# Two FFN projections of a hybrid decoder step as seven half-depth block products (Strassen's scheme)

## The chip, the cores and the metric

The kernel runs on one core of a Trainium2 chip. A core has a matrix engine (TensorE, in the profile PE, with its weight loads as PEld), a vector engine (DVE), an activation engine (ACT), a general engine (POOL), and a queue engine (SP) that issues nearly all transfers here. Each engine takes its instructions in the order in which the program emits them. The metric is the device time of one execution in microseconds, the median of several runs.

## The reference, cut to what matters

The step takes 2048 prompt tokens and 32 sample tokens through one layer: a mixer (an S5 scan and gated linear attention), then a gated FFN with a short causal convolution. The change touches the FFN alone (x has 1024 columns, D_FF is 2816, all float32):

```python
    x = x + jnp.concatenate([y5, o], axis=-1) @ w_o

    h2 = rms_norm(x, ffn_norm)
    a, b = jnp.split(h2 @ w_up, 2, axis=-1)
    ext = jnp.concatenate([conv0.astype(a.dtype), a], axis=1)
    a_conv = conv_b
    for w in range(CONV_W):
        a_conv = a_conv + conv_w[w] * ext[:, w:w + T]
    x = x + (jax.nn.silu(a_conv) * b) @ w_down
    ...
    y_prompt = rms_norm(xp, final_norm)
```

## The kernel before

Every float32 operand of a matmul is held as the sum of a high and a low part on a shorter grid, and every product is three matmuls: high by high, high by low, low by high (`Acc.mm3`). The splitting is vector work: ACT or POOL copies the high part, DVE or POOL subtracts it for the low part.

The program emits a main stream of matmul blocks and, between them, steps of generators that stand in the background (`Background.tick`, `drain`). A coarse clock of the program's own decides only where a step is put; what is emitted is a fixed order for each engine. SBUF is shared out as 43 large slots and 6 small ones (`Slots`); a background generator starts only when enough slots are open.

Four windows of 512 tokens go through the mixer (PSUM banks `mm`, background banks `bg`). The S5 mixer works by halves of 1024 tokens and four groups of channels. When the FFN begins, the S5 of the second half is still to be done: four scans (`gen_s5`), then a gate for pairs of chunks (`gen_glu`, data through the DRAM arrays `ydT` and `gdT`), then the output projection in two halves of columns (`gen_wo`, from `x1d` to `x2d`, eight tiles and a sample tile each). These run in the background of the FFN's first half; all FFN sums and these use the banks `all`.

The FFN of before runs by halves of the tokens. `x2_slots` takes 16 slots (when 17 are open) for the normalized, transposed and split activations `X2H`, `X2L`, which `gen_build` makes tile by tile while the first FFN blocks already run. `FORDER` then goes over the 22 column blocks of D_FF: `ffn_up` makes a and b for a block (8 contraction tiles by 3 matmuls each, windows of 512 tokens in the first half, 352 in the second), convolves and gates; after every second block `ffn_down` adds that pair's share of the down projection to the residual `x2`, which stays in SBUF:

```python
            a = Acc(pa[:, :n], 3 * KD)
            for k in range(KD):
                a.mm3(wv(ab[0], 0, k), wv(ab[0], 1, k), X2H[k][:, s:e], X2L[k][:, s:e])
```

The work of the second half's S5 must be over before the last two blocks of the first half (`bg.drain(*s5[1], *stages[1])`), and `gen_finish` norms and stores the tiles at the end.

Of the kernel before, what the change touches and what calls it, by code (L numbers as in the profile page):

```python
# [124 lines left out]
class Share:  # L125
    """slots that a generator has set aside, so that it can run to its end"""
# [19 lines left out]
def _names(x):  # L146
    """the parts of a tile that x touches"""
# [14 lines left out]
class Free:  # L162
    """a wait for the last use of a tile, not for its data"""
# [5 lines left out]
class Banks:  # L169
    """a wait for the next n background banks"""  # L170
# [5 lines left out]
class Clock:  # L176
    """A coarse estimate of when each engine is free and each tile is written; it only orders the
    instruction streams."""
# [14 lines left out]
    def span(x):  # L193
        """is x in DRAM, its tensor, its first and its last element"""
# [3 lines left out]
    def split_tile(self, t, period, edges):  # L198
        """track parts of the columns of a tile"""
# [5 lines left out]
    def reuse(self, key, t):  # L205
        """a new tile in the place of an old one"""
# [73 lines left out]
class Engine:  # L280
    """nc.<engine> with every call noted in the clock"""
# [56 lines left out]
class Background:  # L338
    """Generators whose steps are set between the blocks of the main matmul stream. A step yields
    what its successor waits for: tiles that TensorE reads, an engine whose backlog counts, or  # L340
    "idle" for something that another part of the program has yet to emit."""
# [14 lines left out]
    def when(self, e):  # L356
        """the time at which the step of e may start"""
# [18 lines left out]
    def relieve(self):  # L376
        """a step that may free memory for the main stream"""
# [6 lines left out]
    def start(self, g, n):  # L384
        """the first n steps of a generator"""
# [4 lines left out]
    def need(self, slots, n):  # L390
        """run steps until n slots are free that nobody has set aside"""
# [3 lines left out]
    def tick(self, most=None):  # L395
        """steps that are ready, for at most so much of TensorE's time"""
# [14 lines left out]
    def drain(self, *gs):  # L411
        """run the generators to their end, others in their waits"""
        while any(e[3] is g for e in self.gens for g in gs):
            if self.tick(1.0):
                continue
            for e in sorted(self.gens, key=lambda e: (self.when(e), e[0], e[1])):
                if self.run(e):
                    break
            else:
                raise RuntimeError("stuck")  # L420
# [3 lines left out]
def kernel(ctx: ExitStack, tc: tile.TileContext, ins, outs):  # L424
# [32 lines left out]
    gdT = drp.tile([2, 4, P, 8, NCH], F32, tag="gdT", name="gdT")  # L457
    x1d = drp.tile([TP + NSMP, D], F32, tag="x1d", name="x1d")
    x2d = drp.tile([TP + NSMP, D], F32, tag="x2d", name="x2d")

# [5 lines left out]
    kept = set()         # banks of sums that the background must go round  # L466
# [7 lines left out]
    clock.next_banks = next_banks  # L474

# [1807 lines left out]
```

## Time and profile before

| | |
|---|---|
| median of 3 runs | 2483.21 us (2483.13 to 2484.64) |
| span of the profiled execution | 2482.2 us |
| PE busy | 2380.4 us, 96% |
| PE weight loads busy | 2032.0 us, 82% |
| DVE busy | 1392.0 us, 56% |
| ACT busy | 678.7 us, 27% |
| POOL busy | 667.5 us, 27% |
| chain that ended last | PE 74%, DVE 7%, POOL 5%, ACT 3% |

The profiled execution is within 1 us of the median. All calls of an engine go through one helper, so every instruction stands under line 290; groups are told apart by the names of tiles (`t_L` a large slot, `t_H` a small one, `pair_L` half of a large one, `all`, `mm` and `bg` PSUM banks) and by shapes. The mean duration of a matmul holds its way through the pipeline; what a matmul of a long row costs is its group's busy time divided by its count.

### The profile page before, as it was taken

The page shows a single profiled execution, that of the slowest core. Times are in us where ns is not written, and L with a number is a line of the kernel's source. Part 1 is how long each engine was busy: PE and PEld are TensorE (multiplying, and loading weights), DVE is VectorE, ACT ScalarE, POOL GpSimd, SP SyncE. Part 2 cuts the span into 40 slices and gives each one's busy share as a digit, 9 for nine tenths or more (in the row PEclk, how much of TensorE's full clock was granted, in tenths as well). Part 3 has the DMA queues.
Part 4 walks back from the last instruction along what each step waited for, and adds up shares of the span by engine and source line. Part 5 has one row for each costly group of instructions (what it writes and reads, how often), then busy time and mean ns, then how long its engine had stood idle before and what let it go on. Part 6 is the DMA issues. An engine that isn't in the chain of part 4 may idle for free.

```text
span 2482.2 us, 32287 instructions
## 1 busy us (share of the span) xinstructions
PE 2380.4 (96%) x12363; PEld 2032.0 (82%) x12363; DVE 1392.0 (56%) x2652; ACT 678.7 (27%) x1401; POOL 667.5 (27%) x761
## 2 busy tenths in 40 slices
PE   7898999899999998999999999999999999999998
PEld 5677777677877877788888888878999999999997
DVE  7677457765633555554445444457555555555555
ACT  3242244444422622223421111154111111111113
POOL 5255325545402344541111001113111011111112
PEclk9889999989999999999999999999999999999999
DMA  6135455427454522233233311136111111111111
GB/s 166 60 96 139 134 152 166 124 86 222 134 178 126 206 77 55 65 94 103 76 113 125 109 51 51 43 101 209 43 43 52 49 37 51 45 41 51 44 34 74
DMA packets 272793, 237.35 MB, mean 96 GB/s; under 512 B 46242, under 2 KB 219482, under 8 KB 272640
## 3 DMA queue, kind: packets, MB, share of 16 engines
q1 hardware_dynamic: 272288, 235.15, 31.5%
q8 instruction: 97, 1.59, 0.3%
q14 instruction: 56, 0.46, 0.1%
q10 hardware_dynamic: 352, 0.15, 0.0%
HBM read 189.16 MB, written 46.09 MB: 95 GB/s over the span
## 4 chain that ended last, share of the span: by engine, by line
PE 74%; DVE 7%; POOL 5%; ACT 3%; issue 1%; DMA 1%; SPq 0%; POOLq 0%; DVEq 0%; ACTq 0%
PE all L290 56%; PE mm L290 11%; PE bg L290 8%; DVE t_L L290 3%; DVE t_H L290 3%; POOL t_H L290 2%; ACT t_L L290 2%; DVE pair_L L290 2%; POOL t_L L290 1%; ACT t_H L290 1%; POOL pair_L L290 1%; POOL rr L290 0%; ACT L290 0%; SPq L290 0%; DMA pair_L<-in_x_prompt_dram 0%
## 5 line engine op out<-in xcount | busy, mean ns | idle before, releaser
L290 PE MATMUL all<-t_L,t_L 128*128 128x512 f32 (+3 forms) x7936 | 1571.2, 360 | 11.2 <-DVE t_L L290 7.5
L290 PEld LDWEIGHTS all<-t_L,t_L 128*128 128x128 f32 x7936 | 1376.3, 187 | 195.2 <-DVE t_L L290 10.2
L290 POOL TENSOR_SCALAR t_L<-t_L 128x1024 fp32r<-128x1024 f32 (+1 forms) x179 | 233.4, 1309 | 1077.8 <-PE all L290 638.1
L290 PE MATMUL mm<-t_L,t_L 128*128 128x512 f32 (+2 forms) x2160 | 494.8, 386 | 18.2 <-DVE t_L L290 14.9
L290 PEld LDWEIGHTS mm<-t_L,t_L 128*128 128x128 f32 (+1 forms) x2160 | 385.2, 192 | 104.4 <-issue 19.5
L290 DVE TENSOR_TENSOR t_L<-t_L,all 128x512 f32<-128x512 f32 (+1 forms) x374 | 249.5, 683 | 168.9 <-PE all L290 158.3
L290 DVE TENSOR_TENSOR t_L<-t_L,t_L 128x1024 fp32r<-128x1024 f32 (+1 forms) x192 | 249.9, 1320 | 48.1 <-POOL t_L L290 24.6
L290 DVE SCALAR_TENSOR_TENSOR t_H<-all,cw,t_H 128x351 f32<-128x351 f32 (+4 forms) x222 | 140.7, 634 | 137.0 <-ACT t_H L290 136.2
L290 ACT ACTIVATE t_H<-all,cw 128x352 f32<-128x352 f32 (+3 forms) x111 | 77.1, 695 | 370.0 <-PE all L290 369.8
L290 DVE TENSOR_TENSOR t_H<-t_H,all 128x352 f32<-128x352 f32 (+3 forms) x112 | 65.5, 585 | 178.2 <-PE all L290 150.9
L290 DVE TENSOR_TENSOR t_L<-t_H,t_L 128x512 fp32r<-128x512 f32 (+5 forms) x171 | 96.3, 579 | 108.4 <-ACT t_L L290 73.3
L290 ACT ACTIVATE t_L<-t_H 128x512 fp32r<-128x512 f32 (+3 forms) x155 | 80.8, 531 | 223.8 <-DVE t_H L290 181.7
L290 ACT ACTIVATE t_H<-t_H 128x352 f32<-128x352 f32 (+4 forms) x113 | 62.1, 550 | 272.2 <-DVE t_H L290 215.3
L290 POOL TENSOR_TENSOR t_L<-t_L,t_L 128x1024 fp32r<-128x1024 f32 x44 | 118.3, 2691 | 44.4 <-ACT t_L L290 32.5
L290 ACT ACTIVATE t_L<-t_L 128x1024 fp32r<-128x1024 f32 (+5 forms) x104 | 95.4, 932 | 62.4 <-DVE t_L L290 30.5
L290 PE MATMUL bg<-t_L,t_L 128*128 128x512 f32 (+6 forms) x604 | 103.9, 339 | 2.3 <-DVE t_H L290 2.3
L290 PEld LDWEIGHTS bg<-t_L,t_L 128*128 128x128 f32 (+3 forms) x604 | 81.3, 184 | 22.0 <-issue 8.4
L290 ACT ACTIVATE t_H<-all 32x512 f32<-32x512 f32 (+1 forms) x26 | 14.9, 575 | 239.1 <-PE all L290 239.1
L290 ACT ACTIVATE t_L<-bg 128x512 fp32r<-128x512 f32 (+6 forms) x118 | 52.6, 466 | 90.1 <-PE bg L290 87.5
L290 ACT ACT_TABLE_LOAD x43 | 55.2, 1283 | 50.4 <-DVE aprev L290 31.5
L290 ACT ACTIVATE t_H<-t_L 128x1024 bf16<-128x1024 f32 (+2 forms) x59 | 57.2, 974 | 34.9 <-DVE t_L L290 23.8
L290 POOL TENSOR_SCALAR rr<-ss 128x1 f32<-128x1 f32 (+1 forms) x51 | 25.0, 490 | 143.0 <-ACT t_H L290 137.8
(173 smaller groups left out, 1646.4 us busy)
## 6 DMA issues: line engine op xcount, KB each, us to landing
t_L<-in_w_up_dram SPq DMA_DIRECT2D x88, 512.0 KB, 4.2
t_L<-in_w_in_dram SPq DMA_DIRECT2D x64, 512.0 KB, 4.9
t_L<-in_w_down_dram SPq DMA_DIRECT2D x44, 512.0 KB, 3.3
t_L<-in_w_o_dram SPq DMA_DIRECT2D x24, 512.0 KB, 5.0
t_L<-x2d SPq DMA_DIRECT2D x24, 512.0 KB, 4.5
out_dram<-t_L SPq DMA_DIRECT2D x17, 512.0 KB, 2.7
t_L<-in_x_prompt_dram SPq DMA_DIRECT2D x16, 512.0 KB, 6.5
t_H<-gdT SPq DMA_DIRECT2D x24, 256.0 KB, 4.1
```

The costliest lines, as they stand in the source:

```text
L290: r = fn(*args, **kw)
```

## The change

The FFN is rewritten. The prompt and sample tokens are cut into three chunks of 704, 704 and 672 columns (`CH`), each chunk into two halves of tokens and the model width into two halves; the weight block of a and b is the other two-by-two matrix. Seven products of half depth (4 contraction tiles, 12 matmuls of 352 or 336 columns) take the place of eight, in the order `PO`; two accumulate on banks of earlier ones. The up projection runs over all 22 blocks of each chunk first; gated rows are stored to the DRAM array `gT`. Then the down projection runs in four parts of the contraction (4, 6, 6, 6 blocks of D_FF) over eight pairs of token tiles, with the residual read from and written to `x2d` in each part.

The last fence of the diff's hooks (`p == 5`) is that of the down projection, where `G` is POOL. Operands are sums and differences of blocks. Those of the activations (up) and of w_down (down) are 21 held slots (`R`), made once for a chunk or part; those of the other side are made for each block (`Item.step`).

```diff
-        hi, lo = ([S.get("L", F32R) for _ in range(KD)] for _ in range(2))
-        for i in half_tiles(0):
-            build[i] = bg.add(3, gen_build(i))
+            bg.need(S, 29)
+        if R or S.open() < 29:
+            return
+        for p in PO:
+            R[p] = [S.get("L", F32R) for _ in range(3)]
+        bg.start(bg.add(3, gen_raw(0)), 1)
+        for i in chunk_tiles(0):
+            build[0, i] = bg.add(3, gen_build(0, i))
+        build["first"] = bg.add(3, gen_first_chunk())
...
+    W.share.end()
+    FW = Share(S, 12.0)
+    FS = Share(S, 4.0)
+    KH = (2, 3, 3, 3)
+    K0 = (0, 4, 10, 16)
+    items = [("up", c, fb) for c in range(3) for fb in range(NF)]
+    items += [("down", q, j) for q in range(4) for j in range(8)]
...
+            if at == 0:
+                self.pair(ra, 1, 2)
+            elif at == 1:
+                ew(self.s[:, h : 2 * h], rb[:, :h], rb[:, h : 2 * h], ALU.add)
+                ew(self.s[:, :h], self.s[:, h : 2 * h], ra[:, :h], ALU.subtract)
+            elif at == 2:
+                self.pair(self.s, 6, 5)
+            elif at == 3:
+                ew(self.s[:, :h], ra[:, h : 2 * h], self.s[:, :h], ALU.subtract)
+                ew(self.s[:, h : 2 * h], ra[:, :h], rb[:, :h], ALU.subtract)
+            elif at == 4:
+                self.pair(self.s, 3, 7)
...
+    def products(it, hook, part, n, kh, out, tail=None):
+        for p in PO:
+            wh, wl, _ = it.take(p)
+            if p in (1, 6, 5, 7, 3):
+                B[p] = bank("up", True)
+            b = B[{2: 1, 4: 7}.get(p, p)]
+            for k in range(kh):
+                for w_, x_ in ((wh, xh), (wh, xl), (wl, xh)):
+                    lh, rh = (w_[:, c], x_) if out == "w" else (w_[:, c], x_)
+                    PE.matmul(b[:, :n], lh, rh, start=i == 0 and p not in (2, 4), stop=i == n_ - 1, skip_group_check=p in (2, 4))
+            if tail:
+                tail(p)
+            after(lambda p=p: hook(p, B))
+            prepare()
+            bg.tick()
...
+            elif p == 5:
+                add(Vv, U, B[5])
+                add(r2[:, hi], r2[:, hi], Vv, G)
+                add(r1[:, hi], r1[:, hi], Vv, G)
+                add(r2[:, lo], r2[:, lo], U, G)
...
+    bg.drain(*(build.pop(k) for k in list(build)))
+    for n, (kind, c, j) in enumerate(items):
+            if j == NF - 1:
+                bg.drain(*(s5[1] + stages[1] if c == 0 else []), *nxt)
+                last = next_window(c + 1) if c < 2 else next_operands(0)
+            up(it, last)
```

`ew` puts an elementwise operation on DVE or POOL by the program's clock, `split2` makes the high part on ACT and the low part with `ew`, `tail` makes the next chunk's or part's operand of a product when the last block has used the old one.

The change also sets another order at the places below. The first is PE at the FFN's start. Before: `mm` is the mixer's last sum, rows with `ident` are transposes that build activations, `all_7016` is the first FFN product.

```order
L290 MATMUL mm_6923<-t_L_6817,t_L_6657 128x512
L290 MATMUL bg_6939<-ident,t_L_6806 128x128 x4
...
L290 MATMUL bg_6979<-ident,t_L_6811 128x128 x4
L290 MATMUL all_7016<-t_L_6666,t_L_6823 128x384
...
L290 MATMUL all_7016<-t_L_6669,t_L_6824 128x384
L290 MATMUL all_7030<-ident,t_L_6869 128x128 x4
L290 MATMUL all_7043<-ident,t_L_6869 128x128 x4
L290 MATMUL all_7016<-t_L_6670,t_L_6823 128x384
```

PE at the same place in the changed kernel, where the first product is `all_7114`:

```order
L290 MATMUL mm_6826<-t_L_6742,t_L_6656 128x512
L290 MATMUL all_6900<-ident,t_L_6824 128x128 x4
L290 MATMUL all_6909<-ident,t_L_6824 128x128 x4
...
L290 MATMUL all_6998<-ident,t_L_6980 128x128 x4
L290 MATMUL all_7016<-ident,t_L_7007 128x128 x4
L290 MATMUL all_7025<-ident,t_L_7007 128x128 x4
L290 MATMUL all_7114<-t_L_6780,t_L_6861 128x352
L290 MATMUL all_7114<-t_L_6781,t_L_6861 128x352
```

Before, the transposes of later tiles stood between the matmuls of the first product; now those of all six tiles of the first chunk stand ahead of it.

The second place is SP's queue at the gate of the second half's S5 (`ydT` is read, `gdT` written). Before:

```order
L290 DMA t_L_9328<-ydT 128x4x256
L290 DMA gdT<-t_L_9328 128x4x256
L290 DMA t_L_9497<-ydT 128x4x256
L290 DMA t_L_9525<-in_w_up_dram 128x8x128
L290 DMA t_L_9531<-in_w_down_dram 128x1024
L290 DMA gdT<-t_L_9497 128x4x256
L290 DMA t_L_9659<-ydT 128x4x256
L290 DMA t_L_9789<-in_w_down_dram 128x1024
L290 DMA t_L_9795<-in_w_up_dram 128x8x128
L290 DMA gdT<-t_L_9659 128x4x256
```

SP at the same place in the changed kernel:

```order
L290 DMA t_L_10608<-ydT 128x4x256
L290 DMA gdT<-t_L_10608 128x4x256
L290 DMA t_L_10681<-ydT 128x4x256
L290 DMA gdT<-t_L_10681 128x4x256
L290 DMA t_L_10754<-ydT 128x4x256
L290 DMA gdT<-t_L_10754 128x4x256
L290 DMA t_L_10827<-ydT 128x4x256
L290 DMA gdT<-t_L_10827 128x4x256
L290 DMA t_H_10900<-ysd 32x512
```

The FFN's weight loads that stood between the gate's transfers are gone from there; each load of `ydT` still stands behind the store of the block ahead.

The third place is PE at that gate. Before: `all_9376` and `all_9429` are gate sums, the rows of 512 columns are FFN products.

```order
L290 MATMUL all_9368<-t_L_9255,t_L_9129 128x512
L290 MATMUL all_9376<-t_L_9354,t_L_9294 128x256
...
L290 MATMUL all_9376<-t_L_9354,t_L_9301 128x256
L290 MATMUL all_9404<-t_L_9122,t_L_8947 128x512
...
L290 MATMUL all_9420<-t_L_9255,t_L_9129 128x512
L290 MATMUL all_9429<-t_L_9354,t_L_9294 128x256
```

PE in the changed kernel, from the end of block 20 of the first chunk (`all_10353`) to block 21 (`all_11547`); `all_10446` belongs to the last S5 group, `all_10616` and `all_10689` to the gate, `all_11350` to the last output projection, rows with `ident` to the second chunk's activations:

```order
L290 MATMUL all_10353<-t_L_6799,t_L_10289 128x352
L290 MATMUL all_10446<-t_L_10378,t_H_10380 128x128 x4
...
L290 MATMUL all_10616<-t_L_10610,t_L_10598 128x256
...
L290 MATMUL all_10677<-ones,t_H_10614 128x1 x2
L290 MATMUL all_10689<-t_L_10683,t_L_10598 128x256
...
L290 MATMUL all_11350<-t_L_11158,t_L_11346 64x512
L290 MATMUL all_11379<-ident,t_L_11370 128x128 x4
...
L290 MATMUL all_11531<-ident,t_L_11513 128x128 x4
L290 MATMUL all_11547<-t_L_6780,t_L_10338 128x352
```

Before, FFN products stood between the sums of the gate and of the output projection; now none stands between the two blocks, and the last S5 group, the whole gate, the whole output projection and six tiles of building do.

## Rows read from the trace of the kernel before

**Rows 1.** Busy time by windows: length, PE, PEld, DVE, ACT, POOL, PEclk, DMA, GB/s

```profile
835.00:2472.00 1637.00, 1611.43 (x8283) 1420.58 (x8283) 874.61 (x1680) 372.38 (x742) 311.22 (x406) 0.99 0.23 71
...
1700.00:2400.00 700.00, 700.00 (x3937) 652.83 (x3936) 376.30 (x786) 117.02 (x246) 88.83 (x72) 1.00 0.18 55
```

**Rows 2.** Groups by shape, PE: count, busy us, mean ns, idle before

```profile
L290 PE MATMUL all<-t_L,t_L 128*128 128x512 f32 x4320 | 993.7, 390 | 6.8 <-DVE t_L L290 6.8
L290 PE MATMUL all<-t_L,t_L 128*128 128x352 f32 x3168 | 508.1, 322 | 0.0
...
L290 PE MATMUL all<-t_L,t_L 128*128 128x256 f32 x240 | 32.0, 292 | 3.5 <-DVE aprev L290 3.3
```

**Rows 3.** DMA issues: count, KB each, median us to landing

```profile
t_L<-in_w_o_dram SPq DMA_DIRECT2D x24, 512.0 KB, 5.0
t_L<-x2d SPq DMA_DIRECT2D x24, 512.0 KB, 4.5
...
t_H<-gdT SPq DMA_DIRECT2D x24, 256.0 KB, 4.1
...
t_L<-ydT SPq DMA_DIRECT2D x8, 512.0 KB, 5.8
```

**Rows 4.** Timeline of SP, 1150 to 1235 us: start, duration, instruction

```profile
1154.24 0.37 SPq L290 DMA_DIRECT2D gdT<-t_L  x1
...
1174.15 0.37 SPq L290 DMA_DIRECT2D gdT<-t_L  x1
...
1229.03 0.36 SPq L290 DMA_DIRECT2D gdT<-t_L  x1
```

**Rows 5.** Groups by shape, DVE, ACT and POOL

```profile
L290 DVE TENSOR_TENSOR t_L<-t_L,t_L 128x1024 fp32r<-128x1024 f32 x180 | 236.0, 1330 | 43.7 <-POOL t_L L290 24.6 <-ACT t_L L290 19.1
...
L290 POOL TENSOR_TENSOR t_L<-t_L,t_L 128x1024 fp32r<-128x1024 f32 x44 | 118.3, 2691 | 44.4 <-ACT t_L L290 32.5 <-PE bg L290 9.6
...
L290 ACT ACTIVATE t_L<-t_L 128x1024 fp32r<-128x1024 f32 x49 | 59.2, 1222 | 26.4 <-DMA t_L<-in_w_in_dram 16.0 <-DVE t_L L290 5.4 <-DMA t_L<-ydT 3.9
...
L290 DVE TENSOR_TENSOR t_L<-t_H,t_L 128x512 fp32r<-128x512 f32 x66 | 47.5, 733 | 33.9 <-ACT t_L L290 33.8
...
L290 ACT ACTIVATE t_L<-t_H 128x512 fp32r<-128x512 f32 x66 | 40.3, 629 | 119.1 <-DVE t_H L290 77.3 <-DMA t_H<-gdT 35.0 <-PE all L290 5.9
...
L290 DVE TENSOR_TENSOR t_H<-t_H,all 128x352 f32<-128x352 f32 x66 | 34.4, 522 | 91.8 <-PE all L290 90.5 <-ACT t_H L290 1.3
...
L290 DVE SCALAR_TENSOR_TENSOR t_H<-all,cw,t_H 128x351 f32<-128x351 f32 x44 | 25.5, 579 | 64.5 <-ACT t_H L290 64.5
...
L290 DVE SCALAR_TENSOR_TENSOR t_H<-all,rrn,t_H 128x512 f32<-128x512 f32 x16 | 12.0, 751 | 48.0 <-PE all L290 48.0
```

**Rows 6.** Timeline of all engines, 812 to 850 us

```profile
835.09 0.44 PE L290 MATMUL all<-t_L,t_L 128*128 128x384 f32 x1 [0.20 <-ACT t_L L290]
...
838.62 1.22 ACT L290 ACTIVATE t_H<-t_L 128x1024 bf16<-128x1024 f32 x1
...
842.97 1.04 ACT L290 ACTIVATE t_H<-t_L 128x1024 bf16<-128x1024 f32 x1
```

**Rows 7.** Timeline of POOL, 850 to 930 us

```profile
860.01 0.89 POOL L290 TENSOR_TENSOR t_H<-t_L,t_L 128x128 f32<-128x128 f32 x2 [10.88 <-ACT t_L L290]
...
868.05 2.09 POOL L290 TENSOR_SCALAR t_L<-t_L 128x1024 fp32r<-128x1024 f32 x2
...
900.47 0.52 POOL L290 TENSOR_TENSOR t_L<-t_L,t_H 128x128 f32<-128x128 f32 x1
```

**Rows 8.** Busy time by windows near the start, columns as in rows 1

```profile
60.00:70.00 10.00, 0.22 (x1) 0.00 (x0) 7.61 (x23) 6.33 (x9) 1.45 (x1) 0.74 0.46 157
70.00:80.00 10.00, 9.06 (x31) 7.30 (x32) 9.93 (x9) 1.89 (x2) 9.85 (x5) 0.75 0.05 6
```

**Rows 9.** Timeline of DVE, 855 to 912 us

```profile
864.51 0.67 DVE L290 TENSOR_TENSOR t_H<-t_L,t_L 128x128 f32<-128x128 f32 x2
...
868.12 2.19 DVE L290 TENSOR_TENSOR t_H<-t_L,t_L 128x128 f32<-128x128 f32 x2 [2.19 <-POOL t_L L290]
```

More of the change, by code (lines that the diff above doesn't have):

```diff
@@ L1174, in gen_s5 @@
             yield "idle"
-        while live[0] >= s5_width[0] or S.open() < 6.5 or (hf and not X2L):
+        while live[0] >= s5_width[0] or S.open() < 6.5 or (hf and not R):
             yield "idle"
@@ L1645, in rows_of, with spans, ew, split2 @@
         return (TP, NSMP) if i == 16 else (i * P, P)
-    def h2_transpose(t, rows, col):
+    def spans(c, i):
+        r0, r = rows_of(i)
+        c0, n = CH[c][0], width(c)
+        out = []
+        for j in range(2):
+            lo, hi = max(r0, c0 + j * n), min(r0 + r, c0 + j * n + n)
+            if lo < hi:
+                out.append((lo - r0, hi - lo, j, lo - c0 - j * n))
+        return out
+    def ew(out, a, b, op):
+        n = 1
+        for d in out.shape[1:]:
+            n *= d
+        e = V if max(clock.eng["V"], clock.eng["PE"]) + 0.07 + 1.04e-3 * n <= max(clock.eng["G"], clock.eng["PE"]) + 0.12 + 2.15e-3 * n else G
+        tt(out, a, b, op, e)
+    def split2(hi, lo, src):
+        act(hi, src, AF.Copy)
+        ew(lo, src, f(hi), ALU.subtract)
+    def gen_raw(c):
+        while (c == 1 and not all(("p3", h, 1, j) in flags for h in (1, 2) for j in [16] + list(range(8)))) or raw or S.open() < 7.0:
+            yield "idle"
+        raw.extend(S.get("L") for _ in range(6))
+        for t in raw:
+            clock.split_tile(t, SL, (0, XN, 2 * XN, 3 * XN, SL))
+    def gen_build(c, i):
+        r0, r = rows_of(i)
+        while not raw or ("split", c - 1) not in flags or not all(("p3", h, int(i > 7), j) in flags for h in (1, 2) for j in ([16] if i == 16 else range(8))) or S.open() < 2.0:
+            yield "idle"
+        S_ = Share(S, 1.5)
+        t = S_.get("M")
+        SP.dma_start(t[:r, :D], x2d[r0 : r0 + r])
+        yield t
+        yield from norm_tile(t[:r, :D], t[:r, :D], r, None, S_)
+        yield t, Banks()
         for q in range(2):
@@ L1685, with gen_operands, gen_first_chunk @@
+    def gen_operands(c):
+        for p in PO:
+            operand(p, width(c), 4, xpc, rawx)
+            yield "V"
+        S.put(*raw)
+        raw.clear()
+        flags.add(("split", c))
+    def gen_first_chunk():
+        yield from gen_diff(0)
+        yield from gen_operands(0)
     p3 = [0]
@@ L2065 @@
     bg.most = MOST[4]
[L2066 to L2082 removed]
+    bg.drain(conv)
@@ new lines, with load_item, prepare @@
+    live_items, loaded = [], [0]
+    def load_item():
+        if loaded[0] < len(items) and len(live_items) < 3 and FW.left >= 2.0 and S.whole() >= 2:
+            it = Item(loaded[0])
+            it.load()
+            live_items.append(it)
+            loaded[0] += 1
+    def prepare():
+        for it in live_items[:2]:
+            if it.at < 6:
+                if FW.left >= it.need() and S.whole() >= it.need():
+                    it.step()
+                break
+        load_item()
@@ new lines, in up, with yp_, gen_raw_down @@
+        products(it, hook, xpc, n, 4, "w", last)
+    def yp_(p, k, r, n):
+        return R[p][k][:, 512 * r : 512 * r + 512]
+    def gen_raw_down(q):
+        while raw or S.open() < 7.0:
+            yield "idle"
+        kh = KH[q]
+        raw.extend(S.get("L") for _ in range(2 * kh))
+        for k, t in enumerate(raw):
+            clock.split_tile(t, SL, (0, 512, SL))
+            SP.dma_start(t[:, :D], w_down[(K0[q] + k) * P : (K0[q] + k + 1) * P, :])
+        for k in range(kh):
+            yield raw[k], raw[kh + k]
+            b12, b22 = (raw[i * kh + k][:, 512:1024] for i in range(2))
+            ew(b12, b22, b12, ALU.subtract)
@@ L2222, in conv_states @@
         S.put(*co)
[L2224 to L2249 removed]
+    for _ in range(2):
+        load_item()
@@ L2250 @@
+    after()
     bg.drain(*ends)
```

515 lines of the change are left out of this document (322 added, 193 removed).

## The prediction

> **What bounds the kernel now.** I read the busy time by windows first. From the first FFN product at 835 us [rows 6] to the last at 2472 us PE is busy 1611 of 1637 us, and from 1700 to 2400 us all of the time, with DVE at 54%, ACT at 17% and POOL at 13% [rows 1]. So the FFN is bound by PE's work; the other engines have room, and the 26 us in which PE was idle there lie where the second half's S5 still runs beside the FFN. Then I read the groups by shape for what a matmul costs: 993.7 / 4320 = 0.230 us for 512 columns, 508.1 / 3168 = 0.160 for 352, 32.0 / 240 = 0.133 for 256 [rows 2]. Last, since the change takes away the cover of what ran in the background, I read the timelines of that work.
>
> The sum is made against the span, 2482 us; the median of the runs is 1 us longer.
>
> **PE's work: -180 us.** Before, the FFN's products are 2016 (up) and 2112 (down) matmuls of 512 columns, 3168 of 352, 96 of 384 (0.175 each, an estimate by columns between the 352 and 512 rows) and 48 of 256: 949 + 508 + 17 + 6 = 1481 us. After, each of 66 up blocks has 7 x 12 = 84 matmuls: 3696 of 352 and 1848 of 336 (0.153, by columns from the 352 row), and the down projection has 8 x 7 x 3 x (2 + 3 + 3 + 3) = 1848 of 512: 593 + 283 + 425 = 1301 us. The sample's 112 small matmuls become 110. This is 12% of the products, and no waiting can make it larger.
>
> **The start of the FFN: +35 us.** The held slots now need 29 open instead of 17, and PE's order has all 48 transposes of six tiles, then the first product. Nothing stands beside them. A tile's building repeats every 842.97 - 838.62 = 4.35 us in the trace [rows 6]; six make 26, the load of the first takes 4.5 [rows 3], and the operands of the first block (28 splits and 12 sums) come a little slower than its products, some 5 more. Were only the last two tiles exposed, it would be 15; with two weight splits ahead on ACT and DVE (1.2 and 1.3 each [rows 5]) and slots that come late, 50.
>
> **The hole between blocks 20 and 21 of the first chunk: +180 us.** This is the largest new term. The second chunk begins at token 704 and so needs second-half tokens, whose S5 must be done when 22 blocks of about 13.5 us have passed; before, it had until the last blocks of the first half. The held operands leave about six large slots, so the S5 groups run one at a time, and the order shows the last scan, the whole gate, the whole output projection and six tiles of building between two FFN blocks. I add up the chain by its rows:
> - The last S5 group, 44 us. Its scan lasted 41 us in the trace, from 860 to 901, with FFN work between [rows 7]; alone I take 26, for 37 POOL steps at 0.5 with some waits on DVE, and 18 for PSUM copies, the closing matmuls, the stores and their landing (estimates from the ACT and DMA rows).
> - The gate, 4 x 17.3 = 69 us: a load of 5.8 [rows 3], high part 1.2 and low part 1.3 [rows 5], 48 matmuls at 0.133 = 6.4, and 2.5 for sigmoid, product and the store's issue. The next load stands behind that store in SP's queue, so nothing overlaps. Bounds: 14.8 without the closing 2.5; 24.9, the mean spacing of the stores before, (1229.03 - 1154.24) / 3, when FFN work was in between [rows 4].
> - The output projection, 101 us: twice 10 for the weights (load 5.0 [rows 3], scaling about the same), 16 tiles two by two, 8 x (4.1 load [rows 3] + 0.6 + 0.7 split + 12 x 0.230 + 0.75 [rows 5]) = 8 x 9.0, and twice 4.5 for the sample.
> - Six tiles of building, 33 us: 2 for the store to land, a load of 4.5, six times 4.35.
>
> That is 247 us, in which PE has 192 x 0.133 + 192 x 0.230 + about 12 = 82 us of work that it also did before: 165 us idle. I add 15 for the clock: where PE did 0.22 of 10 us of work the granted clock fell to 0.74 on average, that is to 1.2 GHz for part of it, and it was 0.75 in the ten after, when PE was busy again [rows 8]. The hole alternates waits of 3 to 11 us with bursts of 6 us, so up to half of its 82 us may run at that level, +40. Ends: 120 (scan mostly covered, quick gate) and 260 (the gate at 24.9, late slots).
>
> The Trainium skill (Perfetto Trace Analysis, Optimization Strategy) says that where the most-contended engine changes over time, interleaving the regimes may help. The kernel of before does that, S5 beside FFN, and the trace bears it out with 26 us of idle PE in the whole FFN; by that rule the change gives this up, and the hole is its price.
>
> **Changing operands: +35 us.** Six times (two chunks, up to down, three parts) the last block also makes the next operands: 28 splits and 12 sums for a chunk, 21 and 9 of 512 columns for a part. The order gives POOL some 14 of these beside its share of the weights; at 2.691 us per 1024 columns [rows 5] that is about 20 us in a block of 13.5 us (28 in one of 14.5). Half of the excess is caught up in the next block: some 6 us each. Bounds 0 and 80.
>
> **The down projection: +15 us.** In its first part a block is 42 x 0.230 = 9.7 us, and the chain PSUM sum, POOL sum of 512 columns (1.35), PSUM sum must fit in three products of 1.4 us while POOL also splits weights: about 1 us a block. The sample's matmuls wait for a load and a split in four places, 2 us each. Bounds 0 and 40.
>
> **DVE beside PE in the up blocks: +25 us.** For a block DVE has 5 PSUM sums (0.522), 4 convolution steps (0.579), 2 products (0.52), 4 sums of 512 (0.733), 2 low parts of 1024 (1.330) [rows 5] and 8 small ones (0.2, an estimate): 13.1 us, against 84 x 0.160 = 13.5 on PE. Weights are made half a block ahead, so short waits are hidden; but there is hardly room. DVE and POOL also get in each other's way: two DVE steps that took 0.67 us took 2.19 when a 2.09 us POOL operation started just ahead of them [rows 7, 9]. Ends: 0, and 105 (1.6 us in each of 66 blocks).
>
> The Trainium skill (SBUF — State Buffer, The single rule) says that the port pair shared by DVE and GpSimd is an exclusive lock, and a DVE instruction with two SBUF inputs waits out a GpSimd one that reads SBUF. The trace agrees with that pair of rows. By the rule, each of POOL's three operations in a block (about 5.5 us) could hold DVE up by half its length: nearly 3 us, which is the upper end; by the mean durations, in which such waits already are, nothing. I lie nearer the latter, since the DVE steps that read PSUM leave room.
>
> The finish is left at its 10 us, the same steps as before. The sum: -180 + 35 + 180 + 35 + 15 + 25 = +110; 2482 + 110 + 1 = 2593 us.
>
> **Rivals.**
> - *The hole is mostly covered* (faster). The steps of the gate and the projection would overlap across blocks, since every engine runs on as far as its data lets it, and the hole would cost 60 us. With the other terms at their values: -180 + 35 + 60 + 35 + 15 + 25 = -10, 2473 us; were the changes of operands hidden too, 2438. It decides below 70 us of hole. For it: in the trace the like steps are mixed with others and their own length is hard to see. Against it: the load of `ydT` stands behind the store of the block ahead, and the gate's stores were 20 to 31 us apart even so [rows 4].
> - *DVE becomes the bound of the up blocks.* By the port waits and in-order waits on ACT each block takes 15.1 us instead of 13.5: +105 instead of +25, 2673 us. For it: 13.1 of 13.5 us [rows 5] and the pair of rows 9. Against it: mean durations overlap a little on DVE, and half a block of weights is ready ahead.
> - *The products are not saved* because each block waits for its weights or banks as long as the eighth product took. Then -180 becomes near 0, 2770 us. Against it: eight banks for five sums, and loads of 1 MB per 13.5 us, which the queues carried before.
>
> **How the numbers follow.** The forecast has 0.70, with 2520 to 2660 of its own; DVE as the bound 0.15; the hole covered 0.10 (nearly all of the faster side); products not saved 0.05. The range 2490 to 2690 leaves out most of the last two. A measurement of this kernel tells about 0.2%, 5 us, from no change: faster 0.09, same 0.02, slower 0.89.
>
> **What would show it.** After: about 1300 us of FFN products in the groups by shape; a stretch near 1190 to 1440 us with PE at a third and `ydT`, `gdT`, `x1d` the releasers; some 30 us without products after 830; short dips of PE at the six changes; PE at 95% or more between them. I am wrong if that stretch is shorter than 150 us, if PE is idle for a fixed share of every up block (then DVE binds), or if matmuls of 352 columns cost other than 0.160 us.

## The result, and the profile after

The changed kernel takes 2950.4 us (median of 4 runs, 2948.6 to 2951.6) against 2483.2 us before: a ratio of 1.189, with a 95% interval from 1.187 to 1.191. The forecast was 2593 us with a range from 2490 to 2690. The sign was right; the loss is 467 us instead of 110. The profiled execution of the changed kernel has a span of 2949.7 us.

First the busy time of the engines by windows, read off PE's timeline: the columns are those of [rows 1]. A block is the 84 matmuls of one of the 22 column blocks of D_FF; the hole is the stretch without FFN products between blocks 20 and 21.

```profile
835.00:876.00 41.00, 8.98 (x48) 7.94 (x48) 13.15 (x37) 20.75 (x43) 7.47 (x14) 0.62 0.53 155
876.00:923.40 47.40, 28.09 (x136) 23.95 (x136) 37.59 (x52) 21.68 (x46) 28.19 (x28) 0.79 0.14 45
923.40:1295.60 372.20, 308.29 (x1772) 302.98 (x1772) 305.21 (x517) 145.71 (x228) 175.73 (x160) 0.90 0.32 94
1295.60:1568.70 273.10, 129.46 (x534) 100.79 (x534) 71.26 (x142) 62.81 (x121) 41.62 (x71) 0.69 0.30 96
1568.70:1610.55 41.85, 25.07 (x123) 24.21 (x121) 36.74 (x52) 20.68 (x42) 26.73 (x21) 0.79 0.16 47
1610.55:1953.90 343.35, 307.72 (x1812) 298.05 (x1812) 273.70 (x480) 152.66 (x258) 96.55 (x64) 0.96 0.31 94
1953.90:1993.10 39.20, 20.04 (x85) 18.74 (x85) 34.03 (x51) 17.45 (x38) 22.94 (x17) 0.68 0.17 49
1993.10:2330.10 337.00, 298.98 (x1766) 289.99 (x1766) 284.52 (x567) 131.89 (x234) 78.03 (x43) 0.93 0.29 91
2330.10:2357.60 27.50, 16.04 (x67) 14.14 (x66) 25.64 (x39) 11.59 (x25) 17.66 (x13) 0.80 0.32 109
2357.60:2492.10 134.50, 99.87 (x370) 72.83 (x370) 77.45 (x110) 38.05 (x70) 78.64 (x64) 0.84 0.56 184
2492.10:2643.10 151.00, 124.83 (x516) 96.86 (x516) 86.08 (x116) 39.29 (x61) 74.57 (x53) 0.93 0.50 165
2643.10:2794.50 151.40, 128.69 (x535) 101.16 (x535) 97.73 (x122) 41.88 (x66) 81.05 (x57) 0.94 0.54 176
2794.50:2938.10 143.60, 132.30 (x543) 102.87 (x543) 109.64 (x114) 60.02 (x90) 108.69 (x83) 0.94 0.43 139
```

In this order they are: the tiles of the first chunk; block 0; blocks 1 to 20; the hole; block 21 with the next operands; blocks 22 to 42 (chunk 1); block 43 with the next operands; blocks 44 to 64 (chunk 2); block 65 with the first down operands; the four parts of the down projection. A border lies where PE's wait for new operands ends, some 36 matmuls into a block. So the windows hold 120 up matmuls with block 0, then 1644, none in the hole, 121, 1763, 85, 1765 and, for the end of block 65, 46. The table sets each against its products at the matmul times of before; what is left over is the "rest", beside the rest that the forecast's terms give.

| stretch | us | products | rest | forecast of the rest |
|---|---|---|---|---|
| tiles and block 0 | 88 | 19 | 69 | 35 |
| blocks 1 to 20, S5 beside | 372 | 264 | 108 | 24 (8 for DVE, 16 for S5's matmuls) |
| hole | 273 | 0 | 273 | 262 (247 and 15 for the clock) |
| blocks 21, 43, 65 | 109 | 40 | 69 | 18 |
| chunk 1, 21 blocks | 343 | 283 | 60 | 8 |
| chunk 2, 21 blocks | 337 | 270 | 67 | 8 |
| down projection | 580 | 425 | 155 | 58 (15, three changes of 6, 25 for the sample) |

The rests sum to 801 us against 413; the 388 between them are 30 more than the 358 by which the span missed the forecast, since small work and waits that the forecast carried over from before stand inside these stretches now. The hole came out near its forecast, 11 us longer. The others did not: up blocks +195, changes of operands and down projection +148, the start +34.

PE's groups by shape, which answer to [rows 2]:

```profile
L290 PE MATMUL all<-t_L,t_L 128*128 128x352 f32 x3696 | 664.3, 342 | 152.3 <-DVE t_L L290 82.3 <-POOL t_L L290 35.2 <-ACT t_L L290 34.9
L290 PE MATMUL all<-t_L,t_L 128*128 128x512 f32 x2040 | 518.1, 414 | 112.1 <-ACT t_L L290 72.0 <-DVE t_L L290 30.6 <-POOL t_L L290 9.4
...
L290 PE MATMUL all<-t_L,t_L 128*128 128x336 f32 x1848 | 317.5, 335 | 50.0 <-POOL t_L L290 33.0 <-ACT t_L L290 14.7 <-DVE t_L L290 2.2
```

A matmul of 352 columns takes 664.3 / 3696 = 0.180 us instead of 0.160, one of 512 0.254 instead of 0.230. In the windows above the granted clock is below 1 in every stretch, so part of PE's work ran at 1.2 GHz instead of 2.4; and PE sat idle for 314 us in front of these three shapes, where before it was idle for 7 [rows 2].

Now a steady block. The next rows are from the timeline of all engines in chunk 1 (start, duration, instruction), and answer to [rows 9].

```profile
1810.28 2.40 POOL L290 TENSOR_TENSOR t_L<-t_L,t_L 128x1024 fp32r<-128x1024 f32 x1 [5.45 <-ACT t_L L290]
...
1810.83 2.40 DVE L290 TENSOR_TENSOR t_L<-t_L,t_L 128x512 fp32r<-128x512 f32 x1 [0.67 <-ACT t_L L290]
1812.73 13.15 PEld L290 LDWEIGHTS all<-t_L,t_L 128*128 128x128 f32 x82 [0.59 <-POOL t_L L290]
...
1819.88 1.29 POOL L290 TENSOR_TENSOR t_L<-t_L,t_L 128x512 f32<-128x512 f32 x1 [7.20 <-DVE t_L L290]
1820.16 1.03 DVE L290 SCALAR_TENSOR_TENSOR t_L<-aprev,cw,t_L 128x1 f32<-128x1 f32 x1
```

POOL's low part of 1024 columns runs from 1810.28 to 1812.68. DVE's low part of 512 columns starts in it, and ends 0.55 us after it. Nine microseconds later a DVE step on one column starts in POOL's sum of 512 columns and ends with it. Between 1760 and 1950 us there are 12 such blocks, and it is so in each: the 12 low parts took 2.36 to 2.43 us, the 12 steps on one column 0.97 to 1.03. Groups by shape and the list of waits there:

```profile
L290 DVE TENSOR_TENSOR t_L<-t_L,t_L 128x1024 fp32r<-128x1024 f32 x24 | 29.3, 1222 | 13.2 <-ACT t_L L290 13.2
L290 DVE TENSOR_TENSOR t_L<-t_L,t_L 128x512 fp32r<-128x512 f32 x12 | 28.9, 2406 | 7.8 <-ACT t_L L290 7.8
...
L290 DVE SCALAR_TENSOR_TENSOR t_L<-aprev,cw,t_L 128x1 f32<-128x1 f32 x12 | 12.0, 1004 | 0.0
```

```profile
DVE t_L L290 <- ACT t_L L290: 30.0, 42, 0.9
...
PE all L290 <- POOL t_L L290: 15.4, 12, 1.8
PE all L290 <- ACT t_L L290: 2.4, 5, 0.7
```

DVE waits for ACT and for nothing else, never for PE. In these 190 us it is busy for 159.8 and waits for 30.0: a block of 15.9 us is 13.4 us of DVE and 2.5 us of its waits. PE, whose products need 13.5, is the one that waits. At 15.9 us the seven products take longer than eight would have taken at the old rate, 96 x 0.160 = 15.4 us.

### The profile page after: what moved, and what is told of

It is laid out like the page before. It is cut to its first block, busy times and chain, and to the rows that moved or that the text cites. A ratio compares the mean times of both kernels' runs of the same rounds, so it can differ in the third digit from the quotient of the medians.

```text
span 2949.7 us, 34921 instructions
## 1 busy us (share of the span) xinstructions
PE 2394.0 (81%) x12345; PEld 2061.6 (70%) x12345; DVE 1963.2 (67%) x3346; ACT 1056.6 (36%) x1937; POOL 1184.5 (40%) x1025
## 5 line engine op out<-in xcount | busy, mean ns | idle before, releaser
L290 PE MATMUL all<-t_L,t_L 128*128 128x352 f32 (+4 forms) x7910 | 1572.6, 361 | 355.2 <-ACT t_L L290 140.6
L290 PEld LDWEIGHTS all<-t_L,t_L 128*128 128x128 f32 (+1 forms) x7910 | 1400.4, 202 | 521.6 <-DVE t_L L290 141.2
L290 POOL TENSOR_TENSOR t_L<-t_L,t_L 128x512 f32<-128x512 f32 (+10 forms) x440 | 739.3, 1693 | 1008.3 <-ACT t_L L290 503.6
L290 DVE TENSOR_TENSOR t_L<-t_L,t_L 128x1024 fp32r<-128x1024 f32 (+11 forms) x774 | 818.0, 1075 | 301.6 <-ACT t_L L290 202.9
L290 ACT ACTIVATE t_L<-t_L 128x1024 fp32r<-128x1024 f32 (+8 forms) x766 | 554.0, 754 | 1027.7 <-DVE t_L L290 449.9
L290 DVE TENSOR_TENSOR t_L<-t_L,all 128x352 f32<-128x352 f32 (+3 forms) x530 | 300.8, 571 | 75.4 <-ACT t_H L290 28.6
L290 POOL TENSOR_SCALAR t_L<-t_L 128x1024 fp32r<-128x1024 f32 (+1 forms) x47 | 71.9, 1537 | 102.2 <-DMA t_L<-in_w_in_dram 44.5
L290 DVE SCALAR_TENSOR_TENSOR t_L<-t_L,cw,t_L 128x351 f32<-128x351 f32 (+3 forms) x132 | 74.3, 563 | 42.4 <-ACT t_L L290 42.4
L290 ACT ACTIVATE t_L<-all 128x352 f32<-128x352 f32 (+5 forms) x147 | 68.4, 469 | 49.0 <-PE all L290 43.0
L290 DVE SCALAR_TENSOR_TENSOR t_L<-all,cw,t_L 128x351 f32<-128x351 f32 (+3 forms) x132 | 75.2, 570 | 8.1 <-ACT t_L L290 7.3
```

Source lines behind the costliest of these rows:

```text
L290: r = fn(*args, **kw)
```

## Experiments

Theory A: the up blocks are bound by DVE, because it stands behind POOL's operations with two inputs. Rivals: DVE is simply full (B); only POOL's late low part stops PE (C); the matmuls themselves are slow. Each kernel below is the changed kernel with the edit shown, cut to what matters, each timed in 4 runs; all stay slower than before, and the interval of the ratio to the kernel before is given. The planner is the program's own clock, by which `ew` chooses an engine and background steps are placed; an edit can shift its choices, and where it did the text says so.

**POOL out of the FFN's shared operations.**

```diff
-        e = V if ... else G
-        tt(out, a, b, op, e)
+        tt(out, a, b, op, V)
```

> Every FFN elementwise operation that was shared between DVE and POOL goes to DVE; POOL keeps S5, the finish and the three sums of a down block. In a steady up block (chunk 1 of the changed kernel: 15.9 us) DVE gets 1.23 + 0.69 = 1.9 us more. Theory A (DVE stands behind POOL's operations: 2.41 instead of 0.73 and 1.00 instead of 0.21 us, 2.5 us a block): these 2.5 us go, the block falls slightly, to 15.0 to 15.5 us, and the operand changes (28, 26 and 15 us beyond a block) shrink; 2860 to 2900 us in all. Rival B (no such waits; DVE is simply full): the block grows to 17.5 us or more, 3020 us or more. Rival C (PE waits only because POOL's low part takes 2.4 us where DVE needs 1.23): the block falls to 14 us, 2800 us.

3027.4 us, ratio 1.217 to 1.222. The blocks of chunk 1 take 15.6 us, those of chunk 2 16.0: just above A's range, far from B (17.5) and from C (14). DVE has 1.9 us more to do in a block and is less busy. Ten blocks of chunk 1, columns as in [rows 1]:

```profile
1845.30:2001.30 156.00, 142.94 (x842) 134.31 (x842) 125.32 (x251) 60.37 (x90) 0.00 (x0) 1.00 0.29 91
```

That is 12.5 us of DVE a block, and 3.0 of waits for ACT, against 13.4 and 2.5 in the changed kernel. So POOL's two operations cost DVE a little more (2.5 us) than they take off it (1.9); and without POOL the block is still 2.1 us above PE's 13.5. DVE's own work with its waits for ACT nearly fills the block even when nothing holds it up. The rest of A's forecast missed. Blocks 43 and 44, where the operands change, take 26 us more than two steady ones (25 in the changed kernel), so the changes did not shrink. The total rose because hardly any S5 work was issued beside chunk 0: its blocks fell to 15.5 us and the hole grew from 273 to 412. The down projection is unchanged at 583.

**One set of weights.**

```diff
+            self.same = self.kind == "up" and (self.c, self.j) != (0, 0)
+            if self.same:
+                self.ready, self.at = samew, 6
```

> Leaves out the loads, sums and splits of all up weights but the first block's: all 66 up blocks use that one's operands. DVE loses 4 sums of 0.68, two low parts of 1.22 and one of 2.41: 7.6 of its 14.7 us a block. If the vector work of the weights is what an up block waits for, chunks 1 and 2 become bound by PE at 13.5 and 12.9 us a block, and with them the granted clock is 1.0: 60 to 67 us less in each of the chunks, some 60 less in chunk 0, in all 2740 to 2790 us. If it is the matmuls themselves (0.171 us instead of 0.160) or the clock, the block stays at 15 us or more and the total above 2880.

2660.8 us, ratio 1.069 to 1.074, below what I expected. In chunk 1 PE is busy for 148.8 of 150 us at a granted clock of 1.00, and 352 columns take 145.0 / 891 = 0.163 us. So the products are saved once the weights' vector work is gone, and it is that work that an up block waits for. S5 fitted beside the blocks as well: the hole is 178 us.

**No convolution sums in chunks 0 and 1.**

```diff
-            for j in (1, 2):
+            for j in (1, 2) if c == 2 else ():
```

> Leaves out the four shifted convolution sums and the four small edge sums of each up block in chunks 0 and 1 (chunk 2 is as it was). DVE loses 2.3 + 1.6 = 3.9 us a block. If DVE as a whole is the bound, chunk 1 falls from 16.3 us a block to PE's 13.6, chunk 2 stays at 16.0, in all about 2950 - 60 - 60 = 2830 us. If the block waits for the weight chain (ACT high part, POOL low part, PE) whatever DVE else does, chunk 1 stays at 15.5 us or more and the total above 2920.

2841.6 us, ratio 1.141 to 1.147, as expected of DVE as the bound: 13.5 us a block in chunk 1, 15.9 in chunk 2, which was not edited. The edit took more off DVE than the convolution, though: in chunk 1 the planner now gave DVE the low part of 1024 columns and POOL that of 512, so the low part that took 2.41 us is off DVE too. One row of the busy time by windows, in chunk 1:

```profile
1660.00:1850.00 190.00, 190.00 (x1185) 190.00 (x1185) 146.66 (x228) 90.56 (x130) 28.64 (x16) 1.00 0.34 105
```

PE is never idle, the clock is 1.00 throughout, and a matmul takes 190 / 1185 = 0.160 us, as before [rows 2]. The slower matmuls of the changed kernel follow from PE's waits; they are no cause.

**ACT copies in POOL's place.**

```diff
+        if e is G and FFN_:
+            act(out, a, AF.Copy)
...
+        else:
+            tt(out, a, b, op, e)
```

> Each FFN operation that POOL did in the changed kernel (a low part of 1024 columns and a sum of 512 in a steady up block) becomes an ACT copy of its first input (the subtraction or sum is left out there); DVE's operations stay. ACT gets 1.06 + 0.62 us a block and has room for it (6.7 of 15.9). Theory A (DVE stands behind POOL): DVE's 512 column low part falls from 2.41 to about 0.73 us, its one-column edge sum from 1.00 to 0.21, the block from 15.9 to 13.7 to 14.2 us in chunks 1 and 2; operand changes shrink to about 10 us; in all 2700 to 2780 us. Rival (DVE is full and waits for ACT by turns, without POOL): those two stay above 1 us or the block at 15.4 us and more, the total above 2890.

2821.7 us, ratio 1.135 to 1.140. DVE's groups in chunk 1, 1750 to 1930 us:

```profile
L290 DVE TENSOR_TENSOR t_L<-t_L,t_L 128x512 fp32r<-128x512 f32 x12 | 8.3, 692 | 18.0 <-ACT t_L L290 18.0
...
L290 DVE SCALAR_TENSOR_TENSOR t_L<-aprev,cw,t_L 128x1 f32<-128x1 f32 x13 | 2.7, 210 | 0.0
```

The same two operations take 0.69 and 0.21 us instead of 2.41 and 1.00, and the blocks fall to 13.5 (chunk 1) and 14.2 us (chunk 2). This shows the mechanism of A: it is POOL's operations that hold these two up. It does not show what POOL is worth on balance, since its work is left out here and not done by DVE; that is read from the first edit. The down projection falls from 580 to 532. The total is above the forecast for A, since S5 was again issued late (hole 410 us).

**More on POOL.** The low part of products 6 and 5 is forced to POOL in the up blocks.

```diff
+            split2(hi[:, : 2 * h], lo[:, : 2 * h], src[:, : 2 * h], G if p0 == 6 and self.kind == "up" else None)
```

> One more low part of 1024 columns a block (that of products 6 and 5) goes from DVE to POOL, in all up blocks; POOL then has about 6 of 15.9 us. If DVE is full and POOL does not hold it up, DVE loses 1.22 us and chunks 1 and 2 fall to 14.7 us a block, total about 2870. If DVE stands behind POOL's operations, one more DVE operation waits 1 to 1.7 us: the block stays at 15.7 us or grows up to 17.5, total 2945 to 3060.

2971.9 us, ratio 1.196 to 1.201. DVE lost 1.22 us a block and took one sum of 0.69 back (the planner's choice), yet the blocks grew, to 16.0 and 16.4 us. A had 15.7 us or more for this and fits; B, which had 14.7, does not.

**One-input operations on POOL.** As the kernel with ACT copies, but POOL makes them.

```diff
+        if e is G and FFN_:
+            ts(out, a, 1.0, ALU.mult, 0.0, ALU.add, eng=G)
...
+        else:
+            tt(out, a, b, op, e)
```

> As the kernel with ACT copies in POOL's place, but the copies (of the first input, the subtraction or sum left out) are made by POOL, as operations with one input. With ACT copies DVE's 512 column low part took 0.69 us, its edge sum 0.21 and a block of chunk 1 13.4 us, against 2.41, 1.00 and 15.9 with POOL's two-input operations. If any POOL operation holds DVE up, the low part takes 1.2 to 2.4 us and the block 14.3 us or more; if only two-input ones do, 0.7 and 13.4 us. Total 2830 to 2900 in the first case, 2800 to 2830 in the second.

2711.6 us, ratio 1.089 to 1.095. The steady blocks take 13.5 and 13.4 us in chunks 1 and 2, and since S5 stayed beside chunk 0 (14.9 us a block on average, hole 306) the total is below both expectations. But the block time doesn't decide between the two readings: the planner gave POOL one sum and one low part a block more than in the changed kernel, so DVE has about 1.4 us less to do. The timeline of POOL and DVE in chunk 2 decides, against the second reading:

```profile
1938.74 0.62 POOL L290 TENSOR_SCALAR t_L<-t_L 128x512 f32<-128x512 f32 x1 [6.10 <-DVE t_L L290]
1939.05 0.32 DVE L290 SCALAR_TENSOR_TENSOR t_L<-aprev,cw,t_L 128x1 f32<-128x1 f32 x1
...
1940.82 1.63 POOL L290 TENSOR_SCALAR t_L<-t_L 128x1024 fp32r<-128x1024 f32 x2 [1.46 <-DVE t_L L290]
1940.98 0.92 DVE L290 COPY sm<-csT 128x16 f32<-128x16 f32 x1
...
1941.91 0.57 DVE L290 COPY cnew<-sm 128x16 f32<-128x16 f32 x1
```

The edge sum ends with POOL's copy here too, and a copy of 16 columns, 0.17 us where POOL was idle, takes 0.92. One-input operations hold DVE up as well. They cost less here because they are short (1.05 us for 1024 columns, against 2.37 for the two-input one) and meet small steps. So the 239 us less than the changed kernel are POOL's slow two-input operations, the waits behind them, and some of DVE's work, together.

**Short operations for POOL, with nothing left out.** All two-input operations on DVE, high parts by turns on ACT and POOL.

```diff
-        tt(out, a, b, op, e)
...
+        tt(out, a, b, op, V)
...
+        if clock.eng["G"] <= clock.eng["A"]:
+            ts(hi, src, 1.0, ALU.mult, 0.0, ALU.add, eng=G)
+        else:
+            act(hi, src, AF.Copy)
```

> Nothing is left out here. All two-input operations of the FFN go to DVE, and POOL makes high parts (copies with one input) by turns with ACT. With two-input operations on DVE and all high parts on ACT a block of chunk 1 had taken 15.6 us, of which DVE was busy 12.4 and waited 3.2 for ACT; its first chunk and the hole behind it took 770 us (693 in the changed kernel). If one-input operations of POOL don't hold DVE up, DVE stays near 12.4 us a block, waits less, and the block falls to 13.6 to 14.8 us; the total is then 2860 to 2960 us. If they do, or if DVE's waits come from its own order, the block stays at 15.5 us or more and the total above 2990.

3010.5 us, ratio 1.210 to 1.216. A block of chunk 1 takes 14.8 us, the end of the first range and 1.1 less than in the changed kernel; in 240 us of it DVE is busy for 213.7 and waits for 25.1 (13.2 and 1.5 us a block). POOL's copies hold it up there too:

```profile
1916.13 1.63 POOL L290 TENSOR_SCALAR t_L<-t_L 128x1024 fp32r<-128x1024 f32 x2 [3.92 <-DVE t_L L290]
...
1917.16 0.97 DVE L290 SCALAR_TENSOR_TENSOR t_L<-t_L,cw,t_L 128x351 f32<-128x351 f32 x1 [0.75 <-ACT t_L L290]
...
1918.19 0.57 DVE L290 SCALAR_TENSOR_TENSOR t_L<-t_L,cw,t_L 128x350 f32<-128x350 f32 x1
```

The first convolution sum starts in POOL's copies and takes 0.97 us, the next, after them, 0.57. The total missed: chunk 2 stays at 15.7, the changes of operands got no shorter, and S5 was issued late again (hole 415). Letting background work run further ahead did not mend that:

```diff
-LIM, LIMP = 9, 2
+LIM, LIMP = 30, 2
```

> The same, and the planner lets background work be issued until DVE or ACT is 30 us ahead of PE in its own reckoning, instead of 9. With all two-input work on DVE that bound had kept S5 out of chunk 0 (410 us of hole instead of 273). If S5 then stands beside chunk 0 again, that chunk and the hole take 690 us or less, the total 80 us less than the kernel without this edit; if S5 needs DVE's time wherever it stands, the two totals differ by less than 30 us.

3042.4 us, ratio 1.224 to 1.230; blocks and hole are the same (416 us), and what is more stands before the first product, which starts at 904 instead of 864 us in the profiled executions (their spans are 39 us apart). So that limit is not what keeps S5 away; that it is the planner's due times against a DVE reckoned full is argued, not shown.

**The hole.** The second chunk's late tiles come from x1d, S5's second half is waited for one chunk later:

```diff
-                bg.drain(*(s5[1] + stages[1] if c == 0 else []), *nxt)
+                bg.drain(*(s5[1] + stages[1] if c == 1 else []), *nxt)
...
+        SP.dma_start(t[:r, :D], (x1d if early else x2d)[r0 : r0 + r])
```

> The second chunk's tiles of the second half are built from x1d (after the attention, before S5's share is added) and don't wait for S5's gate and output projection; these are still done, beside the second chunk, and waited for at its end instead of at the first's. (So the FFN of tokens 1024 to 1407 leaves out S5's share.) Before block 21 of the first chunk the changed kernel has 273 us, of which 82 are PE's own work. If those are latencies that other blocks can cover, the stretch shrinks below 60 us, the second chunk's blocks grow from 16.3 to about 18.6 us as the first chunk's are with S5 beside them, and the total is about 2950 - 190 + 48 = 2810 us. If it is work of DVE, ACT and POOL, which needs its time wherever it stands, the total stays above 2900.

2899.8 us, ratio 1.166 to 1.171: in between. The first gap fell to 46 us (building six tiles), but chunk 1 held only the gate and a part of the projection, and a gap of 112 us stood at its end. Two blocks with a gate step in them take 39.5 us together, so a step costs 39.5 - 2 x 15.9 = 8 us beside blocks instead of 17 alone.

> As the kernel that built the second chunk's late tiles from x1d, but for the third chunk too; the gate and the output projection of the second half are waited for only at the end of the third chunk. (FFN of tokens 1024 and up leaves out S5's share.) There the first stretch had shrunk from 273 to 46 us, but half the projection stood in a second one of 160 us at the end of chunk 1, so that only 50 us were won. If these stretches are latencies that blocks can cover, the second one goes too and some 3 to 4 us a step come back in the blocks: 2780 to 2820 us. If they are vector work, or work that has too few slots beside the blocks, the total stays above 2870.

(The same edit with the third chunk's tiles and `c == 2`. The 160 us of the expectation are those from 1745 us on, where blocks 41 and 42 still stand between the sums of the projection; 112 us of them were without FFN products.) 2835.8 us, ratio 1.140 to 1.144; the gaps before blocks 21 and 43 are 46 and 25 us, and there is none at the end of the third chunk. So 115 of the hole's 191 us of idle (273 less the 82 of PE's work counted ahead) can be covered; the rest comes back as longer blocks. This is between my two expectations, nearer to latency than to work.

**The down projection's operands.** Parts 2 and 3 use those of part 1.

```diff
-            if j == 7 and c < 3:
+            if j == 7 and c < 1:
```

> Parts 2 and 3 of the down projection use part 1's operands; the 8 MB of loads, 42 splits and 18 sums for them are left out. In the changed kernel parts 1, 2 and 3 take 151, 151 and 144 us for 116 us of products and 3 of the sample. If the change of operands costs the 32 us, two of them go: parts 1 and 2 fall to 122 to 130 us, total 2885 to 2905. If the blocks themselves run slower than their products (sums in PSUM's way, weights), the parts stay at 140 us or more, total above 2930.

2896.3 us, ratio 1.165 to 1.169: 54 us less for two changes, 27 each. PE's timeline of the down projection from part 1 on:

```profile
2490.70 27.68 PE L290 MATMUL all<-t_L,t_L 128*128 128x512 f32 x115 [0.73 <-POOL t_L L290]
2522.04 124.00 PE L290 MATMUL all<-t_L,t_L 128*64 128x512 f32 x534 [3.66 <-DVE t_L L290]
2648.65 121.42 PE L290 MATMUL all<-t_L,t_L 128*64 128x512 f32 x534 [2.60 <-DVE t_L L290]
```

Without a change PE runs through a whole part with one wait of 3 us, at 121.42 / 534 = 0.227 us a matmul. What a down block does is hidden; the change is not. The edit leaves out a change's loads, splits and sums together, so which of them costs the 27 us is not shown.

**POOL out of the down projection's sums**, on top of the first edit:

```diff
-                add(r2[:, hi], r2[:, hi], Vv, G)
+                add(r2[:, hi], r2[:, hi], Vv)
```

> The kernel without POOL in the FFN's shared operations, and the three sums of a down block moved from POOL to DVE as well. The first of these two edits alone left the down projection at 583 us (580 in the changed kernel). If POOL's slow sums, and DVE's standing behind them, are what the down blocks wait for, it falls to 540 to 560 us, total 2985 to 3005; if it is the changes of operands and the time of the vector work, it stays at 575 to 600 us, total 3020 to 3045.

3039.1 us, ratio 1.221 to 1.228, 12 more than without it; in the profiled execution the down projection took 604 us against 583. So these three sums are not what the down projection waits for.

## Why the prediction was wrong

**PE's work, -180: right, and not seen.** The products are saved: 0.160 us a matmul and no idle PE where the vector work was lightened enough (the kernel without convolution sums). In the changed kernel itself they are longer by the clock, since PE's waits are spread over all of the FFN. Two of the signs that I had named for being wrong came: PE idle for a share of every up block, and 352 columns at 0.180 us instead of 0.160.

**DVE beside PE, +25: the step that failed most; 195 us more.** I had 13.1 us of DVE work in a block against PE's 13.5 and called it hidden. That DVE was then busy for 13.4 is luck: with POOL idle (the ACT copies) the same DVE steps kept it busy for 10.4 us a block (96.3 of 125 us), so my sum was too high for its own work, and the 2.5 us that POOL holds it up were not in it. What failed is the price of that: I took the nearer end of the range because the mean durations of [rows 5] were said to contain such waits already. Before, POOL had 44 two-input operations of 1024 columns in the whole run [rows 5]; in the changed kernel it has 12 in the 12 blocks above, each at the same place in its block, and the same DVE operation runs into it every time. And the sum left out DVE's in-order waits for ACT, another 2.5 us a block, because "weights are made half a block ahead, so short waits are hidden"; only the rival had them. DVE had 0.1 us left for them.

The range's end was wrong as well. I let POOL's three operations of 5.5 us hold DVE up by half their length; 13.1 and 2.75 are 15.9, 2.4 more than PE's block, some 155 us in 66 blocks, where I wrote 105. POOL has two operations in a block, 3.7 us, and held DVE up for 2.5 of them. The rival that DVE becomes the bound, which I gave 0.15 and 15.1 us a block, is what came, and was still priced too low: 15.9 and 16.0 in chunks 1 and 2, 18.6 in chunk 0. There DVE has S5's steps too and is busy for 15.4 us a block, and these stand behind POOL as well: of 24 sums of 128 columns among them the 12 that met a POOL operation took 1.08 us on average, the 12 that met none 0.28.

The Trainium skill (SBUF — State Buffer, The single rule) says that a DVE instruction with two SBUF inputs waits out a POOL one that reads SBUF, on the port pair they share. The trace agrees: 2.41 instead of 0.69 us and 1.00 instead of 0.21 in every block, and the held steps end with POOL's or just after.

**Changing operands, +35: mis-sized; about 150.** The stretches of blocks 21, 43 and 65 take 22, 26 and 20 us beyond their products, a change between parts 27. I counted POOL's 20 us as the longest and let half of it be caught up. But DVE is busy for 34.0 of the 39.2 us of block 43 and waits for ACT in between, and nothing is caught up in the next block, which is full itself. Its low parts of 336 columns are slowed by POOL as well. The first row is of block 43 in the changed kernel, the second of the same block with ACT copies for POOL:

```profile
L290 DVE TENSOR_TENSOR t_L<-t_L,t_L 128x336 fp32r<-128x336 f32 x20 | 18.2, 958 | 3.5 <-ACT t_L L290 3.5
```

```profile
L290 DVE TENSOR_TENSOR t_L<-t_L,t_L 128x336 fp32r<-128x336 f32 x17 | 8.4, 507 | 6.6 <-ACT t_L L290 6.5
```

With ACT copies for POOL blocks 43 and 44 cost 17 us more than two steady ones, instead of 25; with copies by POOL, 11. But these two kernels also leave work out. With POOL's share done by DVE it is 26, so POOL's holding DVE up is not what makes a change dear; that it is the amount of vector work, which nothing covers, is the likely reading, and no run took it out by itself.

**The down projection, +15: the blocks were nearly right.** Of its 97 us beyond the forecast 63 are three changes at 27 instead of 6. Of the other 34 the first part seems to have most: its steady blocks take 11.4 us for 9.7 of products, and the sample stands in it. That part was not tried alone, so its cause is open.

**The start, +35: 69.** The tiles took 41 us instead of 30, and block 0's stretch 47 us, 28 beyond its products, where I had put 5. DVE is busy there for 37.6 us and POOL for 28.2: its operands cost what a change costs.

**The hole, +180: right, in part by luck.** Net of PE's 82 us it is 191. By its parts: last S5 group 50 (forecast 44), gate 4 x 17.0 (17.3), projection 109 (101), tiles 43 (33). The gate's stores, which answer to [rows 4]:

```profile
1364.97 0.37 SPq L290 DMA_DIRECT2D gdT<-t_L  x1
...
1381.95 0.36 SPq L290 DMA_DIRECT2D gdT<-t_L  x1
...
1399.09 0.36 SPq L290 DMA_DIRECT2D gdT<-t_L  x1
...
1416.05 0.36 SPq L290 DMA_DIRECT2D gdT<-t_L  x1
```

Within a step the errors cancel: in the second one the matmuls took 8.1 us instead of 6.4, the load 4.5 instead of 5.8, what follows the matmuls 1.6 instead of 2.5. The clock's 15 us are in it, and were too few: the granted clock is 0.69 there, and PE was busy for 129 us with work reckoned at 82.

**The range** failed because I gave each uncertain term its likely value and a narrow end, while three of them (the up blocks, the changes, the start) hung on one thing: how little room DVE and POOL have beside PE's shorter products. They moved together, and the total passed every rival's. POOL's holding DVE up is the part of it that was shown by itself, 2.5 us a block; with POOL out of the FFN's shared work the blocks still took 15.6 us and the changes as long as before.

## What to carry to other kernels

When a change moves work from TensorE to the vector engines, add up for one block what DVE does, what it waits for in order, and what it stands behind on POOL, and compare that sum with PE's block, not DVE's busy time alone. Work given to POOL is not gone from DVE: here the 1.9 us that POOL took over cost 2.5. A mean duration from a kernel in which POOL is idle most of the time doesn't contain the waits of one in which POOL works in every block. And when several terms have one cause, the range has to hold the case in which they all go wrong.

## What the runs showed of the hardware

I had not expected that a copy by DVE waits behind POOL as a two-input step does. The copy into `sm` from `csT` in the changed kernel, with ACT copies in POOL's place, and with one-input copies on POOL, whole runs:

```profile
L290 DVE COPY sm<-csT 128x16 f32<-128x16 f32 x22 | 4.3, 196 | 0.0
```

```profile
L290 DVE COPY sm<-csT 128x16 f32<-128x16 f32 x22 | 3.7, 169 | 0.0
```

```profile
L290 DVE COPY sm<-csT 128x16 f32<-128x16 f32 x22 | 19.6, 892 | 0.0
```

DVE's steps that read PSUM kept their time beside POOL. In the changed kernel 43 of the sums of 352 columns ran for over a quarter of a microsecond beside a POOL operation, and took 0.51 us on average as the 174 did that met none.

Nor had I expected how evenly a collision repeats. In a loop whose blocks are all alike the same two instructions meet in each of them: 12 of 12 low parts took 2.4 us, though POOL was busy for only 44.0 of 190 us.
